# First rows of x loaded into the x2 tiles, the first recurrent unit's loads five steps ahead of it, ps_b five steps later, a step between ps_l and ps_g

## The chip, the cores and the metric

One core of a Trainium2 chip runs the whole program in one launch. The metric is the time of one execution on the device in microseconds (us). Engines are named as in the profile: PE is TensorE (matmuls; PEld are its weight loads), DVE is VectorE, ACT is ScalarE, POOL is GpSimd, and SP is SyncE, which only issues transfers. ACT and POOL issue transfers as well.

## The reference

One layer over a sequence of 2048 frames of width 1024, in float32:

```python
h = rms_norm(x, mix_norm_g)
z = h @ w_in                       # 1024 x 3328
z_conv, z_rwkv = z[..., :1536], z[..., 1536:]
y_conv = b_gate * causal_dwconv(c_gate * x_in, conv_mix_w)      # width 3
y_rwkv = rwkv7_mixer(z_rwkv, ...)  # 8 heads of 64, state 64 x 64 per head
x = x + concat([y_conv, y_rwkv]) @ w_out
x = x + conv_glu_ffn(rms_norm(x, ffn_norm_g), ...)              # width 2816
e = rms_norm(p @ ple_w_proj, ple_norm_g)
x = x + sigmoid(rms_norm(x, ple_gate_norm_g) @ ple_w_gate) * e
out = rms_norm(x, final_norm_g)
```

The recurrence in `rwkv7_mixer` takes one frame after the other: `S = S diag(w) + (S (-kk)) (kk a)^T + v k^T`, `out = S r`. Before it come token shift, decay `w`, rate `a` and gate `g` from three small projections; behind it a norm per head, a bonus `sum(r k r_k) v`, and the product with `g`.

## The kernel before

Activations lie transposed, 128 channels by 512 frames; the sequence is cut into four groups (g) of 512 frames. Every dense product is made of three matmuls per block of 128 channels: x and the weights are split into a high part that TensorE takes exactly and a low rest (`hi`, `lo`, three of the four products). A "half" is a weight tile of 128 x 512 with its low part; 12 matmuls use it. In the first group a half comes from HBM as float32 (`raw`, two buffers), ScalarE casts it (`whl` hi, L153), GpSimd subtracts (L154), and SyncE writes both parts back to HBM (`kin`, `ku`, ...). Groups 1 to 3 read these back (L161).

The dense stream runs w_in for the four groups, and then, per group, w_out, the FFN (w_up and w_down, with a piece for the embedding between) and the gate. Beside it runs the recurrent mixer, as a generator `rwkv()`: 16 units of 128 frames (two chunks of 64). The dense generators yield after every half, and `drive` lets `rwkv()` take a step at each yield (0.85 of one in w_out and gate), from the 28th half of w_in on. TensorE's instructions are pinned to this order (`pin`). On the other engines and their issuing queues a scheduler sets the order at build time, by priority and its own account of when operands are there.

A unit has 41 steps. It loads its rows (`rwkv_load`: k, tw, ad, gd, v, r from the scratch `zs`, all issued by SyncE, then kr, sq and three small operations), projects decay and rate (ps_s, ps_a), transposes (ps_n, ps_v; VectorE makes `suv` from ps_v), cumulates the decay (ps_l), projects the gate (ps_g), builds `ari` and `bk`, multiplies them (ps_e, ps_o, with ps_k for the transposes, copied into `tok`), and inverts a triangular matrix per head in a solve of 16 pairs of VectorE instructions (L792, L796), which ends in `dn`. Its rows for unit u + 1 are loaded then. ps_b is the bonus, multiplied into v. Twenty steps behind the load follow gm_ps and x_ps, which complete the inverse, and for each chunk the state (w_ps, u_ps, s_ps, o_ps). All of ps_s to ps_y share the three PSUM buffers of `ps_p`.

Rows of x of group 0 come through `staged` (L203), whose tag "s" has three buffers. The pool `x2`, ten tiles, is used from w_out on only.

```python
RATE = 1.0
SLOW = 0.85
WRAW = 2
NLD = 3
X2 = 10
```

Of the kernel before, what the change touches and what calls it, by code (L numbers as in the profile page):

```python
# [9 lines left out]
F32 = mybir.dt.float32  # L10
# [6 lines left out]
P = 128  # L17
G = 512
# [2 lines left out]
PLE_AT = 2  # L21
HELD = 2
WAIT = 20
R_BONUS = 1
R_POST = 3
R_SCORE = 3
R_MID = 2
R_X = 2
# [34 lines left out]
def tile_trunk(  # L63
# [18 lines left out]
    nc = tc.nc  # L82
    T = xT.shape[2]

    def matmul(*args, **kw):
        return pin(nc.tensor.matmul(*args, **kw))  # L86
# [33 lines left out]
    def v(name, i, n=1):  # L120
        o, _ = VEC[name]
        return vec[:, o + i : o + i + n]
# [72 lines left out]
    def blk(k):  # L195
        return slice(k * P, (k + 1) * P)
# [4 lines left out]
    def staged(pools, src, name):  # L201
        t = pools["tmp"].tile([P, G], F32, tag="s", name=name, bufs=NLD)
        nc.sync.dma_start(out=t, in_=src)  # L203
        return t
# [84 lines left out]

    def in_row(pools, g, rows, k):  # L290
        with tc.high_priority():
            x = staged(pools, xT[k, :, g * G : (g + 1) * G], "x")
        rows.add(pools, x, v("mix_norm_g", k))

    def in_proj(pools, g, rows, nxt):
# [225 lines left out]
    def rwkv_setup(rp):  # L521
        one = rp["one"]
        S = {}
        S["wup"] = one.tile([65, G], F32, tag="wup", name="wup")
        S["aup"] = one.tile([65, G], F32, tag="aup", name="aup")
        S["gup"] = one.tile([P, G], F32, tag="gup", name="gup")
        S["tw"], S["ad"], S["ari"], S["tt"] = [], [], [], []
        for s in range(1):
            for n in ("tw", "ad"):
                t = one.tile([65, P], F32, tag=f"{n}{s}", name=f"{n}{s}")  # L530
                nc.vector.memset(t[64:65, :], 1.0)
                S[n].append(t)
            ari = []
            for par in range(2):
                t = one.tile([P, 4, 2, P], F32, tag=f"ari{par}{s}", name=f"ari{par}{s}")
                ari.append(t)
            S["ari"].append(ari)
            t = one.tile([P, 2, 4, 64], F32, tag=f"tt{s}", name=f"tt{s}")
            nc.vector.memset(t, 0.0)
            S["tt"].append(t)  # L540
        S["e_last"] = one.tile([P, 4], F32, tag="e_last", name="e_last")
        nc.vector.memset(S["e_last"], 0.0)
        S["state"] = one.tile([P, 4, 64], F32, tag="state", name="state")
        nc.vector.memset(S["state"], 0.0)
        return S

    def rest(n):
        for _ in range(n):
            yield

    def rwkv_load(rp, S, u):
        if u >= 4 * NG:
            return None
        g, off = u // 4, (u % 4) * P
        ts = slice(off, off + P)
        r_t, k_t, v_t, kr, sq = (
            rp["t"].tile([P, 4, P], F32, tag="t", name=f"{n}{u}") for n in ("r", "k", "v", "kr", "sq")
        )
        tw, ad = S["tw"][0], S["ad"][0]
        gd = rp["prep"].tile([P, P], F32, tag="gd", name=f"gd{u}")  # L560
        nc.sync.dma_start(out=k_t, in_=zs[g][:, 4:8, ts])
        nc.sync.dma_start(out=tw[0:64, :], in_=zs[g][0:64, 12, ts])
        nc.sync.dma_start(out=ad[0:64, :], in_=zs[g][64:128, 12, ts])
        nc.sync.dma_start(out=gd, in_=zs[g][:, 13, ts])
        nc.sync.dma_start(out=v_t, in_=zs[g][:, 8:12, ts])
        nc.sync.dma_start(out=r_t, in_=zs[g][:, 0:4, ts])
        kkv = v("rwkv_k_k", 0, 4)[:, :, None].broadcast_to([P, 4, P])
        nc.vector.tensor_tensor(out=kr, in0=k_t, in1=kkv, op=ALU.mult)
        nc.scalar.activation(sq, kr, AF.Square)
        nc.scalar.activation(tw[0:64, :], tw[0:64, :], AF.Tanh)  # L570
        nc.scalar.activation(gd, gd, AF.Tanh, scale=0.5)
        nc.gpsimd.tensor_scalar(gd, gd, 0.5, 0.5, op0=ALU.mult, op1=ALU.add)
        return r_t, k_t, v_t, gd, kr, sq

    def rwkv_unit(rp, S, u, loaded, following):
        pr, ch, ps_p, ps_c = rp["prep"], rp["chain"], rp["ps_p"], rp["ps_c"]
        g, off = u // 4, (u % 4) * P
# [12 lines left out]
        def hi_tt(**kw):  # L590
            urgent(tt, **kw)

        def b8(t):
            return t[:, :, None].broadcast_to([P, 8, 64])

        def r8(t):
            return t.rearrange("p (h n) -> p h n", h=8)
# [23 lines left out]
        for ct in range(4):  # L621
# [3 lines left out]
            out=ksum, in_=ps_n.rearrange("p (a h n) -> p a h n", a=4, h=2),  # L625
# [12 lines left out]
        for ct in range(4):  # L638
# [3 lines left out]
            out=mean, in_=r8(ps_v), op=ALU.add, axis=mybir.AxisListType.X  # L642
# [4 lines left out]
        for c in range(2):  # L647
            rs = slice(64 * c, 64 * c + 64)
            pair = []
            for par in range(2):  # L650
# [3 lines left out]
                    out=t[vr], in0=mean4[rs, :, par, None].broadcast_to([64, 4, 64]),  # L654
# [8 lines left out]
        for cp in range(2):  # L663
            ps = ps_p.tile([P, G], F32, tag="p", name="ps_l")
            for c in range(2):
                matmul(
                    ps[:, c * 130 : c * 130 + 130], sg[:, blk(2 * cp + c)], tri[:, 0:130],
                    start=True, stop=True,
                )
            pv = ps[:, 0:260].rearrange("p (a c i) -> p a c i", a=2, c=2)  # L670
            nc.scalar.activation(ep[:, 2 * cp : 2 * cp + 2], pv, AF.Exp, scale=-DECAY)
            nc.scalar.activation(em[:, 2 * cp : 2 * cp + 2], pv, AF.Exp, scale=DECAY)
        ps_g = ps_p.tile([P, 4, P], F32, tag="p", name="ps_g")
        for ct in range(4):
            matmul(ps_g[:, ct, :], S["gup"][:, blk(ct)], gd, start=True, stop=True)
        g_t = big("g")
        nc.scalar.copy(g_t, ps_g)
        yield
        yield

        ari_e, ari_o = S["ari"][s]
# [2 lines left out]
        def cv(t):  # L684
# [9 lines left out]
            out=b_t, in0=tha, scalar=1.0, in1=kr, op0=ALU.add, op1=ALU.mult  # L694
        )
        b4 = cv(b_t)
        for rs, cs in ((E, lo), (O, hi)):
            nc.vector.scalar_tensor_tensor(
                out=bk[rs, :, :, cs], in0=b4[rs], scalar=0.5, in1=em[rs, :, :, 1:65],
# [23 lines left out]

        yield from rest(R_SCORE)
        arb, tok = [], []
# [38 lines left out]
        for pq in range(4):  # L764
            q = pq % 2
            nc.scalar.dma_start(
                out=ld[pq].rearrange("c a i j -> i c a j"),
                in_=ltt[32 * pq : 32 * pq + 32, :, :, 32 * q : 32 * q + 32],
            )
        lm = ch.tile([P, 32, 32], F32, tag="lm", name=f"lm{u}", bufs=1)  # L770
        for r in range(4):
            eng = nc.sync if r % 2 else nc.scalar
            eng.dma_start(
                out=lm[r:P:4].rearrange("m i j -> m (i j)"),
                in_=ld.rearrange("q c a i j -> (q c a) (i j)"),
# [13 lines left out]
        for i in range(0, 32, 2):  # L789
# [3 lines left out]
                out=pd[:, :, :, 0:n], in0=xs[:, :, None, 0:n].broadcast_to([P, 8, 2, n]),  # L793
# [3 lines left out]
                out=xs[:, :, i : i + 2], in_=pd[:, :, :, 0:n], op=ALU.add,  # L797
# [4 lines left out]
            out=xd.rearrange("q n r c i -> (q n r) (c i)"),  # L802
            in_=xs.rearrange("p c i -> p (c i)"),
        )
        dt_ = ch.tile([P, 8, 32], F32, tag="dt", name=f"dt{u}", bufs=1)
        for pq in range(4):
            eng = nc.sync if pq % 2 else nc.scalar
            eng.dma_start(
                out=dt_[32 * pq : 32 * pq + 32], in_=xd[pq].rearrange("n r c i -> (r c) n i")
# [10 lines left out]
        following[0] = rwkv_load(rp, S, u + 1)  # L820
        yield from rest(R_BONUS)
        ps_b = ps_p.tile([P, 4, P], F32, tag="p", name="ps_b")
# [3 lines left out]
        tt(out=v_t, in0=ps_b, in1=v_t, op=ALU.mult)  # L826
        yield from rest(WAIT - R_BONUS)
        gm_ps = ps_c.tile([P, 8, 32], F32, tag="c", name="gm_ps")
# [87 lines left out]
        hi_tt(out=r8(of), in0=r8(of), in1=b8(rs_), op=ALU.mult)  # L916
        yield from rest(R_POST)
        ps_y = ps_p.tile([P, 4, P], F32, tag="p", name="ps_y")
# [13 lines left out]
    pools, rp = {}, {}  # L932
# [13 lines left out]
    S = rwkv_setup(rp)  # L946

    def rwkv():
        following = [None]
        for u in range(4 * NG):  # L950
            loaded = following[0] or rwkv_load(rp, S, u)
            following[0] = None
            yield from rwkv_unit(rp, S, u, loaded, following)
            marks["done"] = u
# [4 lines left out]
    def in_next(g):  # L959
        def run(k):  # L960
            if g < NG and k < KD:
                in_row(pools, g, rows["in", g], k)
        return run

    def out_next(g):
# [5 lines left out]
        return run  # L971

    side = rwkv()
    debt = [0.0]

# [96 lines left out]
```

## Time and profile before

| | |
|---|---|
| median of 3 runs | 2910.98 us (2908.33 to 2916.8) |
| the profiled execution | 2920.32 us |
| its span, first to last instruction | 2918.5 us |
| mean granted clock of TensorE in it | 0.979 of 2.4 GHz |
| first matmul of w_in for group 1 | 194.91 us after the start |

The span is 2 us shorter than the execution's own time. All positions in the trace are microseconds from the start of the span. Matmuls overlap: a matmul of 512 columns is shown as 0.39 us long, but the next one starts sooner than it ends. A clock of 0.50 is the lower of TensorE's two levels, 1.2 GHz.

### The profile page before, as it was taken

To read this page: it belongs to the slowest core of one execution; us is meant where nothing else is said; L and a number is where in the kernel's file an instruction comes from. 1 tells how busy PE (TensorE), PEld (TensorE's weight loads), DVE (VectorE), ACT (ScalarE), POOL (GpSimd) and SP (SyncE) were. 2 spreads that over 40 slices of the span, in tenths; PEclk is the share of its full clock that TensorE was granted. 3 is DMA by queue.
4 is the path that set the end of the run, shared out by engine and by line. 5 is a ranking of instruction groups with operands and counts; after the bars stand their busy time and mean duration, and the time that the engine had idled before them with its cause. 6 is when DMAs were issued, how large, how long until landed. Compare 5 with 4: busy or idle time off the path is not lost.

```text
span 2918.5 us, 42094 instructions
## 1 busy us (share of the span) xinstructions
PE 2771.0 (95%) x15464; PEld 2231.7 (76%) x15464; DVE 1894.1 (65%) x3039; ACT 962.9 (33%) x1721; POOL 1109.2 (38%) x1700
## 2 busy tenths in 40 slices
PE   8899999999889999889999999999999999999997
PEld 6678788778677777667778887777788877788885
DVE  4476656648586768696676677866676856544446
ACT  4333132313453433352513123434222233411113
POOL 4533232324555565552333333323333332333321
PEclk9999999999999999989999999999999999999998
DMA  8787767777776776668665665766665658766665
GB/s 296 263 271 224 231 212 225 208 222 257 243 257 234 239 246 225 229 224 265 188 188 163 193 186 177 227 208 192 186 191 171 183 175 280 220 195 194 190 186 168
DMA packets 285803, 629.97 MB, mean 216 GB/s; under 512 B 60186, under 2 KB 113690, under 8 KB 285596
## 3 DMA queue, kind: packets, MB, share of 16 engines
q0 software_dynamic: 95040, 346.07, 39.4%
q1 hardware_dynamic: 134144, 232.83, 24.4%
q10 hardware_dynamic: 56412, 48.36, 5.2%
q8 instruction: 123, 2.02, 0.3%
q14 instruction: 84, 0.69, 0.1%
HBM read 467.77 MB, written 159.38 MB: 215 GB/s over the span
## 4 chain that ended last, share of the span: by engine, by line
PE 49%; DVE 20%; DMA 16%; ACT 5%; issue 5%; POOL 3%; ACTq 1%; SPq 0%; DVEq 0%; POOLq 0%
PE ps_mm L86 33%; PE ps_d L86 11%; DVE uf L415 3%; DVE pd L792 3%; DMA rawu<-in_w_up 2%; DMA lm<-ld 2%; DVE xs L796 2%; DMA rawin<-in_w_in 2%; DMA x<-in_xT 1%; DVE zb L255 1%; DMA ld<-ltt 1%; DMA xd<-xs 1%; PE o_ps L86 1%; DMA dt<-xd 1%; DMA es<-e 1%
## 5 line engine op out<-in xcount | busy, mean ns | idle before, releaser
L86 PE MATMUL ps_mm<-hi,whlu 128*128 128x512 f32 x2816 | 912.5, 398 | 6.0 <-ACT hi L214 4.2
L86 PEld LDWEIGHTS ps_mm<-hi,whlu 128*128 128x128 f32 x2816 | 535.0, 190 | 123.8 <-ACT hi L214 5.0
L86 PE MATMUL ps_mm<-lo,whlu 128*128 128x512 f32 x1408 | 554.2, 394 | 4.8 <-DVE lo L215 4.8
L86 PE MATMUL ps_mm<-hi,whlin 128*128 128x512 f32 x1664 | 541.7, 399 | 14.9 <-ACT whlin L153 6.9
L86 PE MATMUL ps_d<-hi,whld 128*128 128x512 f32 x1408 | 457.7, 397 | 13.8 <-DVE zb L255 5.9
L86 PEld LDWEIGHTS ps_mm<-hi,whlin 128*128 128x128 f32 x1664 | 316.1, 190 | 87.0 <-ACT whlin L153 6.9
L415 DVE SCALAR_TENSOR_TENSOR uf<-zb,vec,uf 128x512 f32<-128x512 f32 x352 | 291.7, 831 | 111.6 <-ACT uf L410 100.8
L86 PE MATMUL ps_mm<-lo,whlin 128*128 128x512 f32 x832 | 328.3, 395 | 1.6 <-DVE lo L215 1.6
L86 PEld LDWEIGHTS ps_d<-hi,whld 128*128 128x128 f32 x1408 | 266.4, 189 | 77.7 <-DVE x L455 7.0
L410 ACT ACTIVATE uf<-zb,vec 128x512 f32<-128x512 f32 x176 | 143.1, 815 | 526.8 <-DVE zb L255 481.3
L86 PEld LDWEIGHTS ps_mm<-lo,whlu 128*128 128x128 f32 x1408 | 268.0, 190 | 60.3 <-DVE lo L215 6.0
L161 POOL DMA_DIRECT2D whlu<-ku x264 | 141.8, 537 | 422.9 <-PE ps_mm L86 278.3
L86 PE MATMUL ps_d<-lo,whld 128*128 128x512 f32 x704 | 276.3, 392 | 0.0
L255 DVE TENSOR_TENSOR zb<-ps_mm,rstd 128x512 f32<-128x512 f32 x216 | 148.3, 687 | 174.9 <-PE ps_mm L86 174.1
L455 DVE TENSOR_TENSOR x<-ps_d,x 128x512 f32<-128x512 f32 x192 | 131.3, 686 | 139.3 <-PE ps_d L86 138.6
L86 PEld LDWEIGHTS ps_mm<-lo,whlin 128*128 128x128 f32 x832 | 158.1, 190 | 36.8 <-DVE lo L215 5.2
L86 PE MATMUL ps_mm<-hi,whlo 128*128 128x512 f32 x512 | 164.1, 399 | 7.9 <-DVE x L396 5.9
L86 PE MATMUL ps_mm<-hi,whlg 128*128 128x512 f32 x512 | 168.8, 405 | 0.0
L161 POOL DMA_DIRECT2D whlin<-kin x156 | 84.1, 540 | 221.0 <-PE ps_mm L86 182.8
L154 POOL TENSOR_TENSOR whlu<-rawu,whlu 128x512 fp32r<-128x512 f32 x88 | 120.0, 1364 | 109.5 <-ACT whlu L153 102.6
L154 POOL TENSOR_TENSOR lo<-th,hi 128x512 fp32r<-128x512 f32 x88 | 115.6, 1314 | 103.0 <-ACT hi L153 102.4
L86 PEld LDWEIGHTS ps_d<-lo,whld 128*128 128x128 f32 x704 | 133.5, 190 | 25.9
(205 smaller groups left out, 4237.9 us busy)
## 6 DMA issues: line engine op xcount, KB each, us to landing
whlu<-ku POOLq DMA_DIRECT2D x264, 512.0 KB, 4.4
whlin<-kin POOLq DMA_DIRECT2D x156, 512.0 KB, 4.8
whld<-kd POOLq DMA_DIRECT2D x132, 512.0 KB, 4.1
ku<-whlu SPq DMA_DIRECT2D x88, 512.0 KB, 4.4
kin<-whlin SPq DMA_DIRECT2D x52, 512.0 KB, 4.9
whlo<-ko POOLq DMA_DIRECT2D x48, 512.0 KB, 5.5
whlg<-kg POOLq DMA_DIRECT2D x48, 512.0 KB, 4.4
rawu<-in_w_up SPq DMA_DIRECT2D x88, 256.0 KB, 3.5
```

What stands on the lines that cost most here:

```text
L86: return pin(nc.tensor.matmul(*args, **kw))
L154: nc.gpsimd.tensor_tensor(out=lo, in0=raw, in1=hi.bitcast(F32), op=ALU.subtract)
L161: nc.gpsimd.dma_start(out=t, in_=kept[key])
L255: nc.vector.tensor_tensor(out=zb[:, 2 : G + 2], in0=ps, in1=rstd, op=ALU.mult)
L410: nc.scalar.activation(u, zb[:, 2 : G + 2], AF.Identity, bias=v("ffn_conv_b", n), scale=v("ffn_conv_w", 88 + n),)
L415: nc.vector.scalar_tensor_tensor(out=u, in0=zb[:, d : d + G], scalar=v("ffn_conv_w", 44 * d + n), in1=u, op0=ALU.mult, op1=ALU.add,)
L455: nc.vector.tensor_tensor(out=x2[m], in0=ps, in1=x2[m], op=ALU.add)
L792: tt(out=pd[:, :, :, 0:n], in0=xs[:, :, None, 0:n].broadcast_to([P, 8, 2, n]), in1=lm[:, None, i : i + 2, 0:n].broadcast_to([P, 8, 2, n]), ...
L796: nc.vector.tensor_reduce(out=xs[:, :, i : i + 2], in_=pd[:, :, :, 0:n], op=ALU.add, axis=mybir.AxisListType.X,)
```

## The change

Four edits. `R_BONUS` goes from 1 to 6: ps_b comes six steps behind the load of the next unit instead of one; the 20 steps up to gm_ps stay. `yield` between ps_l and ps_g: the two steps that followed ps_g are now one between and one behind. Group 0's rows of x go into eight tiles of `x2`, half issued by ScalarE, half by SyncE. `rwkv()` loads unit 0 first and then rests for five steps, so that every unit comes five steps later.

```diff
--- before.py
+++ after.py
@@ -21,8 +21,9 @@
 PLE_AT = 2
 HELD = 2
 WAIT = 20
-R_BONUS = 1
+R_BONUS = 6
 R_POST = 3
+R_FIRST = 5
 R_SCORE = 3
 R_MID = 2
 R_X = 2
@@ -289,7 +290,12 @@
 
     def in_row(pools, g, rows, k):
         with tc.high_priority():
-            x = staged(pools, xT[k, :, g * G : (g + 1) * G], "x")
+            src = xT[k, :, g * G : (g + 1) * G]
+            if g == 0:
+                x = pools["x2"].tile([P, G], F32, tag="x2", name=f"x0_{k}")
+                (nc.scalar if k % 2 else nc.sync).dma_start(out=x, in_=src)
+            else:
+                x = staged(pools, src, "x")
         rows.add(pools, x, v("mix_norm_g", k))
 
     def in_proj(pools, g, rows, nxt):
@@ -670,12 +676,12 @@
             pv = ps[:, 0:260].rearrange("p (a c i) -> p a c i", a=2, c=2)
             nc.scalar.activation(ep[:, 2 * cp : 2 * cp + 2], pv, AF.Exp, scale=-DECAY)
             nc.scalar.activation(em[:, 2 * cp : 2 * cp + 2], pv, AF.Exp, scale=DECAY)
+        yield
         ps_g = ps_p.tile([P, 4, P], F32, tag="p", name="ps_g")
         for ct in range(4):
             matmul(ps_g[:, ct, :], S["gup"][:, blk(ct)], gd, start=True, stop=True)
         g_t = big("g")
         nc.scalar.copy(g_t, ps_g)
-        yield
         yield
 
         ari_e, ari_o = S["ari"][s]
@@ -946,7 +952,8 @@
     S = rwkv_setup(rp)
 
     def rwkv():
-        following = [None]
+        following = [rwkv_load(rp, S, 0)]
+        yield from rest(R_FIRST)
         for u in range(4 * NG):
             loaded = following[0] or rwkv_load(rp, S, u)
             following[0] = None
```

On PE, the start of unit 0 behind w_in's matmuls, before (names are output and inputs, whlin the weight half):

```order
L86 MATMUL ps_mm<-hi,whlin_0_1005 128x512
L86 MATMUL ps_l<-c_tri,s_951 128x130 x4
L86 MATMUL ps_g<-gd_937,gup 128x128 x4
L86 MATMUL ps_mm<-hi,whlin_1_1012 128x512
L86 MATMUL ps_mm<-lo,whlin_1_1012 128x512
L86 MATMUL ps_mm<-hi,whlin_1_1012 128x512 x2
L86 MATMUL ps_mm<-lo,whlin_1_1012 128x512
```

and in the changed kernel:

```order
L87 MATMUL ps_mm<-hi,whlin_1_1081 128x512
L87 MATMUL ps_l<-c_tri,s_1056 128x130 x4
L87 MATMUL ps_mm<-hi,whlin_0_1166 128x512
L87 MATMUL ps_mm<-lo,whlin_0_1166 128x512
L87 MATMUL ps_mm<-hi,whlin_0_1166 128x512 x2
L87 MATMUL ps_mm<-lo,whlin_0_1166 128x512
...
L87 MATMUL ps_mm<-hi,whlin_0_1166 128x512
L87 MATMUL ps_g<-gd_937,gup 128x128 x4
L87 MATMUL ps_mm<-hi,whlin_1_1173 128x512
```

ps_g has moved behind a whole half (whlin_0_1166), and the unit itself behind five more halves of w_in (row 285 there, row 330 here).

On DVE, around the solve of unit 0 before (fold and lm prepare the matrix, pd and xs are the pairs):

```order
L761 STREAM_TRANSPOSE ltt_1294<-lt_1188 128x512
L826 TENSOR_TENSOR v_934<-ps_b,v_934 128x512
...
L781 TENSOR_TENSOR fold_1305<-lm_1300,c_sq 128x512
L783 TENSOR_TENSOR fold_1305<-fold_1305,lm_1300 128x512
...
L784 TENSOR_TENSOR lm_1300<-lm_1300,fold_1305 128x16x32
L255 TENSOR_TENSOR zb<-ps_mm,xin 128x512
L792 TENSOR_TENSOR pd<-xs_1311,lm_1300 128x16x2
L796 TENSOR_REDUCE xs_1311<-pd 128x8x2
L792 TENSOR_TENSOR pd<-xs_1311,lm_1300 128x16x4
```

and in the changed kernel:

```order
L787 TENSOR_TENSOR fold_1444<-lm_1439,c_sq 128x512
L789 TENSOR_TENSOR fold_1444<-fold_1444,lm_1439 128x512
L790 TENSOR_TENSOR lm_1439<-lm_1439,fold_1444 128x16x32
...
L798 TENSOR_TENSOR pd<-xs_1450,lm_1439 128x16x2
L802 TENSOR_REDUCE xs_1450<-pd 128x8x2
L832 TENSOR_TENSOR v_934<-ps_b,v_934 128x512
L798 TENSOR_TENSOR pd<-xs_1450,lm_1439 128x16x4
L802 TENSOR_REDUCE xs_1450<-pd 128x8x2
```

The product of ps_b with v stood ahead of fold; it now stands behind the first pair, so inside the solve. In the other 15 units it lies between the fold and the seventh pair.

On SP, the first transfers before (rawin is a raw weight half, kin the halves written back):

```order
L203 DMA x<-in_xT 128x512
L168 DMA rawin_0_228<-in_w_in 128x512
L203 DMA x<-in_xT 128x512
L168 DMA rawin_1_235<-in_w_in 128x512
L203 DMA x<-in_xT 128x512
L788 DMA xs_1311<-in_c_tri 128x256
L203 DMA x<-in_xT 128x512
L168 DMA rawin_0_269<-in_w_in 128x512
L171 DMA kin_0_232<-whlin_0_227 128x1024
L203 DMA x<-in_xT 128x512
```

and in the changed kernel (rows named x without a number are already group 1's):

```order
L296 DMA x_0_156<-in_xT 128x512
L204 DMA x<-in_xT 128x512
L169 DMA rawin_0_228<-in_w_in 128x512
L204 DMA x<-in_xT 128x512
L296 DMA x_2_173<-in_xT 128x512
L169 DMA rawin_1_235<-in_w_in 128x512
L204 DMA x<-in_xT 128x512
L296 DMA x_4_191<-in_xT 128x512
L296 DMA x_6_209<-in_xT 128x512
L169 DMA rawin_0_269<-in_w_in 128x512
L172 DMA kin_0_232<-whlin_0_227 128x1024
```

SyncE issues four of group 0's rows among the first nine transfers, with three rows of group 1 between them; the other four are issued by ScalarE.

## Rows read from the trace of the kernel before

**Rows 1.** The page, busy time: us, share of the span, instructions.

```profile
PE 2771.0 (95%) x15464; PEld 2231.7 (76%) x15464; DVE 1894.1 (65%) x3039; ACT 962.9 (33%) x1721; POOL 1109.2 (38%) x1700
```

**Rows 2.** Waits of PE, whole span: us in total, times, longest.

```profile
PE ps_g L86 <- DVE suv L653: 11.0, 7, 3.3
PE ps_n L89 <- ACT sq L569: 10.9, 1, 10.9
PE ps_b L86 <- ACT tok L755: 8.8, 4, 3.8
PE ps_o L86 <- DVE arb L752: 7.8, 5, 4.0
```

**Rows 3.** Windows by stage from 194.9 us to the end, their sum.

```profile
sum 2723.60, PE 2605.57 PEld 2101.84 DVE 1785.22 ACT 884.14 POOL 1018.52; mean PE 200.43 PEld 161.68 DVE 137.32 ACT 68.01 POOL 78.35
```

**Rows 4.** Timeline of ACT, 4 to 26 us: start, us, instruction, idle before.

```profile
5.08 0.63 ACT L227 ACTIVATE sq<-x 128x512 f32<-128x512 f32 x1 [2.61 <-DMA x<-in_xT]
...
15.85 0.63 ACT L227 ACTIVATE sq<-x 128x512 f32<-128x512 f32 x1 [3.83 <-DMA x<-in_xT]
...
23.14 0.71 ACT L214 ACTIVATE hi<-x,vec 128x512 fp32r<-128x512 f32 x1
```

**Rows 5.** The chain that ended last, 95 to 130 us: start, us, what.

```profile
101.15 3.33 DMA rawin<-in_w_in
...
115.51 4.43 DMA v<-zs
```

**Rows 6.** Timelines of SP, POOL and PE, 55 to 195 us.

```profile
55.00 0.33 SPq L168 DMA_DIRECT2D rawin<-in_w_in  x1
...
98.53 0.33 SPq L168 DMA_DIRECT2D rawin<-in_w_in  x1
...
97.22 1.28 POOL L154 TENSOR_TENSOR whlin<-rawin,whlin 128x512 fp32r<-128x512 f32 x1 [0.78 <-ACT whlin L153]
...
98.82 0.39 PE L86 MATMUL ps_mm<-hi,whlin 128*128 128x512 f32 x1
...
194.91 0.47 PE L86 MATMUL ps_mm<-hi,whlin 128*128 128x512 f32 x1 [1.65 <-DMA whlin<-kin]
```

**Rows 7.** Windows: length, busy us (instructions) by engine, granted clock, DMA, GB/s.

```profile
10.00:20.00 10.00, 6.49 (x12) 3.27 (x12) 6.36 (x9) 5.13 (x9) 2.71 (x2) 1.00 0.89 311
...
70.00:80.00 10.00, 10.00 (x45) 8.26 (x44) 3.61 (x4) 3.74 (x6) 5.71 (x7) 1.00 0.89 311
...
120.00:130.00 10.00, 9.92 (x47) 8.53 (x48) 5.66 (x12) 2.63 (x8) 2.10 (x3) 0.83 0.39 125
...
98.40:193.30 94.90, 79.06 (x365) 63.32 (x363) 65.50 (x97) 34.49 (x67) 44.08 (x45) 0.91 0.79 261
```

**Rows 8.** Timelines of PE and DVE, one window: unit 9 at ps_g.

```profile
1437.26 1.74 PE L86 MATMUL ps_g<-gd,gup 128*128 128x128 f32 x8 [3.17 <-DVE suv L653]
...
1448.96 0.69 DVE L711 TENSOR_TENSOR bk<-km,em 64x512 f32<-64x512 f32 x1
...
1454.47 0.37 PE L86 MATMUL ps_e<-ari,bk 64*128 64x128 f32 x1
...
1437.60:1441.00 3.40, 3.40 (x14) 2.92 (x13) 1.86 (x4) 3.26 (x11) 0.00 (x0) 0.50 0.68 237
```

**Rows 9.** Timelines of PE and DVE, one window: unit 5 at ps_b.

```profile
848.91 0.80 PE L86 MATMUL ps_b<-pbh,hones 128*128 128x512 f32 x1 [3.78 <-ACT tok L755]
...
848.90:853.90 5.00, 4.99 (x12) 3.93 (x13) 4.83 (x10) 0.62 (x1) 2.42 (x4) 0.50 0.75 268
...
905.29 0.45 DVE L812 STREAM_TRANSPOSE dn<-dt 128x256 f32<-128x256 f32 x1 [6.97 <-DMA dt<-xd]
...
908.39 0.69 PE L86 MATMUL gm_ps<-dn,lt 32*32 32x32 f32 x32
```

**Rows 10.** Groups by line: busy us, mean ns of one, idle before.

```profile
L792 DVE TENSOR_TENSOR pd<-xs,lm 128x32 f32<-128x32 f32 (+15 forms) x256 | 139.7, 546 | 5.5 <-POOL lm L786 0.9
...
L796 DVE TENSOR_REDUCE xs<-pd 128x16 f32<-128x32 f32 (+15 forms) x256 | 110.6, 432 | 5.2
```

## The prediction

> **What bounds the kernel now.** The page first: TensorE (PE) is busy for 2771.0 of 2918.5 us [rows 1], and its queue keeps the order in which the program was written, so every microsecond that its head waits is added to the time; the other engines matter only where they make it wait. Then the waits of PE by what ended them. The reader should see that three of them belong to places that the diff touches: ps_g, 11.0 us in seven waits, ps_n, 10.9 us in one, ps_b, 8.8 us in four [rows 2]. Then the busy time by stage: after 194.9 us PE is idle for 2723.6 - 2605.6 = 118 us [rows 3]; ps_g and ps_b hold 20 of them, many scattered waits the other 98. The granted clock in such rows shows a second price: behind a long wait PE runs for some microseconds at 0.50, its 1.2 GHz level [rows 8, 9]. Last, the start: ScalarE takes up the first row of x at 5.08 us, stands idle 3.83 us for the load of the fifth, and is done with the eighth at 23.85 us [rows 4]; those loads wait for one of the three "s" buffers.
>
> **First rows of x.** In the change all eight loads are out by about 10 us. What then limits is ScalarE's own order: eight squares of 0.63 us, eight "hi" of 0.71 us, three casts of a weight half ahead of the last "hi" (same size, taken at 0.63), three issues of about 0.33 us: 10.7 + 1.9 + 1.0 = 13.6 us after 5.08, so the last row is ready near 19 us instead of 23.85 [rows 4, 6]. That is 5 us at the first product. I book **nothing** for it. The chain that ended last runs at about 100 us not over PE but over the loop of the weights: a raw half is loaded (3.33 us there), cast, subtracted on GpSimd (1.28 us), and only then comes the next load, as there are two raw buffers [rows 5, 6]. From 55.00 to 98.53 us SyncE issues 15 halves, 2.90 us each [rows 6]; PE's 45 matmuls in 10 us [rows 7] make 2.67 us for the 12 of a half. So PE eats up its lead, and at the 29th half none is left: the subtraction ends at 98.50 us, PE reads what it wrote at 98.82 [rows 6]. A PE that begins 5 us earlier meets the same loop earlier, and the loop begins no earlier: ScalarE now casts the third and fourth halves behind rows of x. Bounds: 5 us won, 2 lost.
>
> The loads also go over two issuing queues now. An issue takes SyncE 0.33 us [rows 6], so four fewer save it 1.3 us, and between 10 and 20 us the DMA engines were 0.89 busy already [rows 7]. The Trainium skill ("DMA: Bandwidth & Descriptors", section "Issuing engines are not separate DMA queues") says that engines which issue DMAs bring no bandwidth of their own, and that issuing on several saves only issue time. By that rule the split is worth at most the 1.3 us; by the rows the wait for buffers that goes is worth 5 us at the first product and none at the 29th half, so the sum is the same by both.
>
> **First recurrent unit.** Its loads stay at the 28th half of w_in, and the unit begins five halves later. Before, PE stood 10.9 us ahead of ps_n [rows 2], and then some 2 us more ahead of ps_v, whose v was issued at 115.51 us and landed 4.43 us later [rows 5]. In the new order k and v each stand two raw loads earlier on SyncE, and PE comes five halves, 13.4 us, later: more than the 13 us of wait. From 98.4 to 193.3 us PE works off 24 halves with 94.9 - 79.1 = 15.8 us idle, at a mean clock of 0.91; in 120 to 130 us the clock was 0.83 and the DMA engines had fallen to 0.39 [rows 7]. A clock of 0.91 over 94.9 us is 17 us at half speed, most of it while PE stood; I count 7 us of work at half speed, 3.5 us lost. Without both, PE would end near 174. The weights allow 98.5 + 24 x 2.90 = 168, plus thirteen loads of 256 KB (k, v and r of two units, rows of x for the next group) at 0.8 us (estimate from the 311 GB/s of [rows 7]): 178. I take 177, a gain of **16 us**. Bounds: 20 if the weights keep up, 6 if those loads count twice (3.3 us a half).
>
> **A step between ps_l and ps_g.** ps_g needs a PSUM buffer that VectorE's (DVE's) instructions suv free. One more half of dense work, 2.67 us, covers a wait of 3.17 us nearly whole. The steps up to ps_e are as many as before, so PE comes there earlier by what it did not wait. In the unit at 1437 us the last bk ends at 1449.65 and ps_e starts at 1454.47, a slack of 4.8 us [rows 8]: nothing is given back there. Three of these waits are followed by a stretch like the 3.4 us at 0.50 in [rows 8], half of each lost: 5 us. So 11.0 + 5 = 16 at most; 5 if the evacuations behind ps_e, for which ps_o waits 7.8 us now [rows 2], take the rest. I book **12**, a microsecond given back in each of four units.
>
> **ps_b five steps on.** It waits for the copy tok; 13.4 us later that is long done. That is 8.8 us, and half of the 5.0 us at 0.50 behind the longest wait [rows 9], 11.3 together. Next late is gm, which needs dn: in that unit dn ends at 905.74 and gm starts at 908.39, so of the 3.78 us only 2.65 are kept [rows 9]. I take off 2.3 in all and book **9** (4 to 11).
>
> The product of ps_b with v moves too, from ahead of the triangular solve on VectorE into it: about 0.69 us (VectorE's time for such a size in [rows 8]) in a chain of 16 pairs of 546 + 432 ns [rows 10]. In the unit of [rows 9] gm has 2.65 us of slack; three or so have none. **2 us lost** (0 to 11, 16 x 0.69, if none had).
>
> **All units five steps later.** By counting steps, no unit is run out of turn: the last of each four still ends before its rows are asked for. But all 16 now lie 13.4 us later against the dense stages, and the 98 us of other waits are dealt anew. No row says which way: 0, with 12 us to either side (an eighth).
>
> Sum: -16 - 12 - 9 + 2 = -35 us. The profiled execution took 2920.3 us, its span 2918.5; the median of the runs, 2911.0, lies 9 us lower, and I take the same 35 us off it: **2876 us**.
>
> **Rivals.** (1) The weights hold PE: at 3.3 us a half the unit's one wait turns into many small ones, and 16 becomes 6: 2886 us. For it: no lead at 98.5 us. Against: the DMA engines' share of 0.39 in 120 to 130 us [rows 7], time that the loop gets back once PE no longer stands. (2) The waits move: VectorE is the late one at ps_g, and what PE gains it loses at ps_o and gm; 21 shrinks to 7: 2890 us. For it: ps_o's 7.8 us; against it, the slacks of 4.8 and 2.65 us. (3) Slower: the solve, 16 x 0.98 = 15.6 us of VectorE per unit [rows 10], slides by 13.4 us from the w_out stage into the start of the FFN, where PE waits for the norm and for the lo of the last row. At the three such starts with a unit running, 15.6 us and 1.7 us of clock each make 52: 2911 - 35 + 52 = 2928 us. It decides from 12 us at each start. Against: VectorE's order mixes dense instructions between the pairs, and a pair lasts 1 us. (4) The change does little: the loads were not what held the first unit, or the weights are late and the other waits come back as well: within 9 us of 2911.
>
> **How the numbers follow.** The forecast (2862 to 2890, from the 12 us of the re-dealing) 0.58; rival (1) 0.15; (2) 0.15; (4) 0.08; (3) 0.04. A measurement of this kernel tells about 0.3%, 9 us, from no change; faster by that are the first three cases, 0.88; the same 0.08; slower 0.04. For 8 in 10 the range takes in (1), (2) and both at once, 2900, and downward the better bounds (20, 16 and 11 us) with part of the re-dealing: 2856.
>
> **What would show it.** Right: ps_n waits for less than 3 us and no 0.50 between 110 and 130 us; the first matmul of the second group's w_in near 178 us instead of 194.91 [rows 6]; ps_g and ps_b gone from the list of PE's waits; small waits of w_in's matmuls for the halves (POOL, ACT whlin) between 45 and 100 us, in which the 5 us of the start go. Wrong: a start of the second group after 188 us; more than 8 us of new waits at ps_o, ps_k and gm; waits of 5 us and more at the starts of the FFN; VectorE waiting for ps_b inside the solve.

## The result and the profile after

The changed kernel takes 2931.03 us (median of 6, 2922.94 to 2937.01), the kernel before beside it 2913.89 us (6 runs, 2908.33 to 2921.87): a ratio of 1.0059, 95% interval 1.0043 to 1.0076. It is slower by 17 us where 35 us faster was forecast. The profiled execution took 2929.27 us; its span is 9.0 us longer than that of before, so the trace shows about half of what the medians show.

The page, busy time, against [rows 1]:

```profile
PE 2775.5 (95%) x15464; PEld 2234.3 (76%) x15464; DVE 1914.6 (65%) x3039; ACT 962.5 (33%) x1721; POOL 1107.1 (38%) x1700
```

The same 15464 matmuls keep PE busy 4.5 us longer, and it is idle 4.5 us longer. VectorE, with the same 3039 instructions, is busy 20.5 us longer. The waits of PE (us in total, times, longest), to be read against [rows 2]:

```profile
PE ps_e L87 <- DVE bk L716: 26.5, 6, 7.7
PE ps_d L87 <- DVE zb L256: 13.6, 7, 2.9
...
PE gm_ps L87 <- DVE dn L818: 7.3, 2, 6.2
...
PE ps_e L87 <- ACT pbh L727: 4.5, 1, 4.5
...
PE ps_o L87 <- DVE bk L717: 3.3, 4, 1.2
...
PE ps_g L87 <- issue: 1.3, 1, 1.3
...
PE ps_g L87 <- DVE suv L659: 0.8, 1, 0.8
```

The three waits at which the edits aimed are gone or nearly gone: ps_n 10.9, ps_b 8.8, ps_g 11.0 to 2.1. In their place stands one that was 1.2 us before: ps_e for `bk`, 26.5 us, the next stop of a unit behind ps_g. The waits of gm_ps for `dn` have grown from 1.4 us, and those of ps_d, a product of w_down, for `zb` from 5.9. Windows (length; busy us and instructions of PE, PEld, DVE, ACT, POOL; clock; DMA; GB/s) from the second group to the end, and of the stretch ahead of it:

```profile
188.06:2927.50 2739.44, 2610.76 (x14762) 2106.16 (x14762) 1808.41 (x2883) 883.99 (x1584) 1016.14 (x1597) 0.98 0.67 210
98.40:188.00 89.60, 81.52 (x377) 64.98 (x375) 62.48 (x88) 34.75 (x67) 45.47 (x45) 0.96 0.87 288
```

The second group begins at 188.06 us instead of 194.91 [rows 6], 6.9 us won, and the stretch ahead of it runs at a clock of 0.96 instead of 0.91 [rows 7]. From there to the end it takes 2739.4 us where it was 2723.6 [rows 3]: 15.8 us lost, 10.7 of them idle time of PE (128.7 against 118.0). Most of this is lost early: w_out of group 0 begins at 707.4 us instead of 703.4, so 10.8 of the 15.8 us go in w_in of groups 1 to 3. One wait there is new, for the end of unit 1's solve:

```profile
355.56 0.64 PE L87 MATMUL gm_ps<-dn,lt 32*32 32x32 f32 x16 [6.23 <-DVE dn L818]
```

### The profile page after: what moved, and what is told of

Its sections match the earlier page's. It is cut to its first block, busy times and chain, and to the rows that moved or that the text cites. A ratio compares the mean times of both kernels' runs of the same rounds, so it can differ in the third digit from the quotient of the medians.

```text
span 2927.5 us, 42080 instructions
## 1 busy us (share of the span) xinstructions
PE 2775.5 (95%) x15464; PEld 2234.3 (76%) x15464; DVE 1914.6 (65%) x3039; ACT 962.5 (33%) x1721; POOL 1107.1 (38%) x1700
## 4 chain that ended last, share of the span: by engine, by line
PE 40%; DVE 14%; DMA 8%; issue 3%; ACT 3%; POOL 2%; ACTq 0%; SPq 0%; DVEq 0%; POOLq 0%
PE ps_mm L87 24%; PE ps_d L87 12%; DVE uf L421 2%; DMA rawu<-in_w_up 2%; DVE pd L798 1%; DMA rawd<-in_w_down 1%; PE ps_e L87 1%; DVE xs L802 1%; DMA out<-o 1%; DMA y<-ys 1%; POOL whlu L155 1%; DVE sq L230 1%; PE o_ps L87 1%; DMA ld<-ltt 1%; DVE zb L256 1%
## 5 line engine op out<-in xcount | busy, mean ns | idle before, releaser
L87 PE MATMUL ps_mm<-hi,whlu 128*128 128x512 f32 x2816 | 912.7, 398 | 14.2 <-ACT hi L215 10.7
L87 PEld LDWEIGHTS ps_mm<-hi,whlu 128*128 128x128 f32 x2816 | 535.3, 190 | 133.5 <-ACT hi L215 12.5
L87 PE MATMUL ps_mm<-hi,whlo 128*128 128x512 f32 x512 | 165.9, 401 | 10.5 <-DVE x L402 6.6
```

## The experiments

Each run gives the ratio of its time to that of the kernel before, measured in turn on the same chip. 0.1% is 2.9 us.

| run | what it is | median, us | ratio (95%) |
|---|---|---|---|
| only_x | before + rows of x at once | 2911.1 | 0.9959 (0.9943 to 0.9974) |
| only_first | before + five steps ahead of unit 0 | 2923.5 | 1.0013 (1.0000 to 1.0025) |
| only_psg | before + step ahead of ps_g | 2911.0 | 0.9961 (0.9945 to 0.9977) |
| only_psb | before + ps_b five steps on | 2923.3 | 1.0008 (0.9994 to 1.0022) |
| no_x | changed, without the rows of x | 2926.7 | 1.0048 (1.0031 to 1.0065) |
| no_first | changed, without the five steps | 2905.6 | 0.9973 (0.9956 to 0.9990) |
| no_psg | changed, without the step ahead of ps_g | 2916.6 | 1.0006 (0.9996 to 1.0016) |
| no_psb | changed, with ps_b in its old place | 2922.8 | 1.0032 (1.0020 to 1.0044) |
| x_psg | before + x + step ahead of ps_g | 2907.8 | 0.9966 (0.9952 to 0.9980) |
| all_early | changed, b, tha and km ahead of that step | 2940.5 | 1.0074 (1.0058 to 1.0090) |
| x_psg_early | x_psg, b, tha and km ahead | 2912.2 | 0.9983 (0.9969 to 0.9996) |
| all_back | changed, five steps given back by unit 4 | 2911.5 | 0.9980 (0.9966 to 0.9994) |
| late4 | no_first, five steps behind unit 3 | 2916.8 | 1.0024 (1.0009 to 1.0039) |
| late8 | no_first, five steps behind unit 7 | 2926.5 | 1.0067 (1.0047 to 1.0087) |
| first10 | changed, ten steps instead of five | 2928.9 | 1.0067 (1.0044 to 1.0089) |
| xg_back | all_back with ps_b in its old place | 2901.2 | 0.9969 (0.9953 to 0.9986) |
| all_lean | changed, fewer products in the gate | 2922.3 | 1.0013 (0.9996 to 1.0029) |
| no_first_lean | no_first, fewer products in the gate | 2901.6 | 0.9944 (0.9922 to 0.9966) |

**One part alone.** Each takes the lines of one edit of the change's diff: `in_row`; `rwkv()` with R_FIRST; the `yield`; R_BONUS.

> The kernel before with the loads of the first rows of x alone changed (all eight into the x2 tiles at once, on two queues). Theory A (as predicted: the weight loop eats what is won at the first product): no change, within 3 us, and the 29th half of w_in begins on TensorE at 98.4 us as before. Theory B (the loads at once stand ahead of the first halves of the weights, and the loop of the raw halves starts later for it): 2 to 4 us slower, and the 29th half begins near 101 us.

> The kernel before with the first unit loaded and then begun five steps on, and nothing else; all 16 units slide by five steps. Theory A (prediction): 16 us faster, with the second group's w_in beginning near 179 us, and what the slide deals anew in the later stages within 12 us of zero. Theory B (the slide puts the preparation of later units under the stretches in which VectorE has a backlog, and loses there more than the first unit gains): the second group begins at 184 to 188 us (7 to 10 us won), but the whole is 5 to 20 us slower than before, the loss being between 190 and 720 us.

> The kernel before with the step between ps_l and ps_g alone (one of the two steps behind ps_g moved ahead of it). Theory A (prediction): 12 us faster, waits at ps_g under 2 us in all, none of over 2 us new at ps_e, ps_o. Theory B (VectorE's backlog sets the moment, and TensorE only waits for it one stop later): ps_g's waits go, but at least two thirds of their 11 us come back as waits of ps_e and ps_o for bk; 0 to 4 us faster.

> The kernel before with ps_b and its product with v five steps on, alone. Theory A (prediction): 7 us faster (9 of waits and clock, 2 lost through the product of v inside the triangular solve), ps_b's waits of 8.8 us gone, gm's waits no more than 3 us longer. Theory B (the wait moves to gm, and the product inside the solve delays dn by 0.7 us and more in each unit): ps_b's waits gone, waits of gm for dn 6 us and more longer; within 3 us of before.

Two parts win 0.4% each, two do nothing that can be told. By their sum, 17 us should be won; together they lose 17. PE in only_x, then in only_first:

```profile
113.47 0.90 PE L89 MATMUL ps_n<-c_sq,sq 128*128 128x128 f32 x3 [4.19 <-ACT sq L574]
...
191.25 0.47 PE L86 MATMUL ps_mm<-hi,whlin 128*128 128x512 f32 x1 [0.77 <-DMA whlin<-kin]
```

```profile
120.03 0.60 PE L90 MATMUL ps_n<-c_sq,sq 128*128 128x128 f32 x4
125.52 1.12 PE L90 MATMUL ps_v<-c_sq,v 128*128 128x128 f32 x4 [4.88 <-ACT s L612]
...
188.60 0.47 PE L87 MATMUL ps_mm<-hi,whlin 128*128 128x512 f32 x1 [1.63 <-DVE pd L793]
```

The five steps do take the whole wait at ps_n, and win 6.3 us up to the second group, not 16: 4.9 us come back at ps_v, which waits for ScalarE's `s`. On ScalarE it stands behind casts of weight halves, one of which waited 4.73 us for its raw half. By 707.7 us, the start of w_out, only_first is 4.3 us late, so it loses 10.6 us between 190 and 708 us, where Theory B put the loss; the whole loss of 4 us lies just under Theory B's 5. The time of only_x fits neither of its theories. The rows of x win 3.7 us up to the second group by themselves, since the wait at ps_n shrinks from 10.9 to 4.2 us: the 29th half does begin 3 us later, as Theory B of only_x said, but k and v stand two raw loads earlier on SyncE's queue (k behind 32 of them instead of 34, in every run with the rows of x and in no other). Both gains are of the same wait: with both parts it is 6.9. Where the other 8 of the 12 us of only_x come from its trace doesn't show: its profiled execution, 2917.1 us, was the longest of its six.

only_psg does what was forecast, 11 us. ps_g's waits fall to 0.7 us; ps_e waits 12.5 us for tok instead of 3.2, in waits of up to 4.8 us, though the forecast had none of over 2 us there; 1.3 us are for bk. So the waits at ps_g move on in large part, and where the 11 us come from isn't shown by them alone. only_psb loses its waits of 8.8 us, and gm waits 10.0 us for dn instead of 1.4: Theory B.

**One part left out.** The changed kernel with the lines of one edit put back.

> The changed kernel with the first rows of x loaded as before through the three s buffers. Theory A (x at once costs nothing): as the changed kernel, within 3 us. Theory B (it holds up the loop of the weights by 2.6 us): 2 to 4 us faster than the changed kernel, the 29th half at 98.4 us.

> The changed kernel without the first unit's five steps: all units stand against the dense stages as they did before. Theory A (the slide is worth 16 us at the start): 10 to 16 us slower than the changed kernel, 2940 to 2948. Theory B (the slide is what loses the time): faster than before, 2895 to 2905, as ps_g and ps_b keep what they won where the units stand as before. Theory C (VectorE's backlog takes back what any moved wait wins): within 4 us of the kernel before.

> The changed kernel with ps_g straight behind ps_l again. Theory A (the step is worth 12 us): 12 us slower than the changed kernel. Theory C (the wait moves from ps_g to ps_e): within 4 us of the changed kernel; waits at ps_g back at 8 us and more, those of ps_e for bk (26.5 us in the changed kernel) smaller by about as much.

> The changed kernel with ps_b one step behind the copies to tT, as before. Theory A (worth 7 us): 7 us slower than the changed kernel. Theory C (the wait moves to gm, or the product of v delays the solve by as much): within 3 us of the changed kernel; gm's waits for dn, 7.3 us in the changed kernel, smaller by 3 us and more.

Without the five steps the kernel is faster than before: in company they cost 0.86%, 25 us, though 4 alone. The step ahead of ps_g, worth 11 us alone, costs 0.53% beside them; without it ps_g waits 12.4 us again and ps_e only 8.6 for bk, so what the step takes from ps_g comes back larger at ps_e. Neither theory of no_psg had it 15 us faster than the changed kernel. The rows of x have no effect that can be told in company. Without the change of ps_b the kernel is 0.27%, 8 us, faster, at the edge of the noise and against both theories: ps_b waits 8.4 us again and gm waits longer, not less (9.7 us instead of 7.3).

From the first matmul of ps_l to that of ps_e a unit with nothing in its way takes 15.5 us. By the timelines, in us (the last column adds what all 16 units take beyond 15.5):

| | unit 4 | 5 | 8 | 9 | 12 | 13 | sum beyond |
|---|---|---|---|---|---|---|---|
| before | 15.9 | 16.0 | 21.6 | 21.4 | 20.6 | 21.5 | 30.7 |
| only_psg | 16.9 | 15.5 | 21.5 | 16.4 | 19.1 | 17.4 | 18.3 |
| only_first | 17.7 | 18.4 | 29.8 | 17.8 | 20.0 | 17.1 | 35.7 |
| no_first | 16.6 | 15.6 | 21.0 | 18.4 | 19.1 | 16.4 | 18.6 |
| all_back | 16.1 | 15.5 | 20.4 | 17.2 | 19.1 | 16.5 | 18.4 |
| changed | 20.1 | 22.7 | 28.7 | 17.9 | 25.0 | 17.9 | 43.9 |
| late4 | 15.5 | 23.1 | 29.4 | 17.9 | 23.0 | 18.3 | 36.7 |
| late8 | 16.2 | 15.5 | 25.9 | 18.6 | 23.1 | 17.9 | 28.7 |
| first10 | 19.4 | 19.4 | 22.1 | 17.1 | 26.8 | 15.6 | 30.1 |
| no_psg | 18.8 | 18.5 | 30.9 | 17.3 | 20.4 | 17.1 | 42.0 |
| all_lean | 19.6 | 21.8 | 23.5 | 17.5 | 19.6 | 17.3 | 31.1 |

The step ahead of ps_g alone takes 12.4 off the sum, about its gain of 11 us, and with the units five steps later the sum is 25 higher, as many us as the five steps cost. But the sum doesn't give a run's time: no_psg has almost the changed kernel's sum and is 15 us faster, and late4, with a sum 8 above that of late8, is 12 us faster than it. Units 8 and 12 prepare at the gate stages, unit 4 at the end of w_in and unit 5 in the FFN. Unit 8, VectorE's timeline in the changed kernel, from the last suv to the last bk:

```profile
1280.93 2.68 DVE L497 TENSOR_TENSOR gt<-raw,rstd 128x512 f32<-128x512 f32 x2
...
1289.96 1.72 DVE L659 SCALAR_TENSOR_TENSOR suv<-mean,ps_v 64x256 f32<-64x256 f32 x4
1291.70 0.69 DVE L501 SCALAR_TENSOR_TENSOR gt<-gt,e 128x512 f32<-128x512 f32 x1
1292.31 0.69 DVE L493 TENSOR_TENSOR e<-e,rstd 128x512 f32<-128x512 f32 x1
...
1300.69 1.78 DVE L699 SCALAR_TENSOR_TENSOR b<-tha,kr 128x512 f32<-128x512 f32 x1
1302.39 1.79 DVE L230 TENSOR_TENSOR sq<-sq 128x512 f32<-128x512 f32 x1
...
1305.29 0.74 DVE L504 SCALAR_TENSOR_TENSOR x<-gt,pg_h,x 128x512 f32<-128x512 f32 x1
1305.95 0.68 DVE L497 TENSOR_TENSOR gt<-ps_mm,rstd 128x512 f32<-128x512 f32 x1
...
1312.39 0.68 DVE L497 TENSOR_TENSOR gt<-ps_mm,rstd 128x512 f32<-128x512 f32 x1
1312.99 1.16 DVE L716 TENSOR_TENSOR bk<-km,em 64x512 f32<-64x512 f32 x1
1314.18 0.69 DVE L717 TENSOR_TENSOR bk<-km,em 64x512 f32<-64x512 f32 x1
```

PE's row behind it, and then the window from suv to bk:

```profile
1314.30 0.76 PE L87 MATMUL ps_e<-ari,bk 64*128 64x128 f32 x2 [7.72 <-DVE bk L716]
```

```profile
1291.70:1314.90 23.20, 15.36 (x70) 12.58 (x70) 22.99 (x27) 10.65 (x25) 14.96 (x12) 0.90 0.64 211
```

The same unit without the five steps (no_first): VectorE's timeline, then the window:

```profile
1258.34 1.75 DVE L492 TENSOR_TENSOR e<-e,rstd 128x512 f32<-128x512 f32 x1
...
1264.97 1.54 DVE L698 SCALAR_TENSOR_TENSOR b<-tha,kr 128x512 f32<-128x512 f32 x1
...
1270.22 1.67 DVE L716 TENSOR_TENSOR bk<-km,em 64x512 f32<-64x512 f32 x1
...
1279.91 1.28 DVE L496 TENSOR_TENSOR gt<-raw,rstd 128x512 f32<-128x512 f32 x2
```

```profile
1257.60:1271.90 14.30, 14.30 (x63) 11.64 (x63) 14.09 (x17) 9.77 (x25) 8.21 (x7) 0.89 0.46 151
```

The reader should see where gt, the gate's first product, stands. It can't start before the gate's norm is there, at 1280.93 and 1279.91 us. Without the five steps the unit's last bk is done 8 us ahead of it (ps_e starts at 1277.83 us and waits for nothing), and 17 instructions of VectorE lie between suv and bk, 14 of them the unit's. With them the unit's preparation begins 11 us behind it, and 27 lie there, 13 of them the gate's (gt, e, x, sq). VectorE is busy for 22.99 of 23.20 us.

**By stage.** That wait of 7.7 us lengthens its stage little: the first gate stage takes 68.0 us in the changed kernel and 65.6 in no_first. The three gate stages together (a fourth ends the kernel), changed and then no_first:

```profile
sum 178.70, PE 162.20 PEld 131.15 DVE 137.97 ACT 87.69 POOL 85.62; mean PE 54.07 PEld 43.72 DVE 45.99 ACT 29.23 POOL 28.54
```

```profile
sum 179.10, PE 161.01 PEld 129.17 DVE 143.35 ACT 86.09 POOL 79.41; mean PE 53.67 PEld 43.06 DVE 47.78 ACT 28.70 POOL 26.47
```

They are no longer in the changed kernel: the wait for bk stands where no_first has other waits. All stages, in us between first matmuls, in one execution of each version, which can lie 8 us off its median:

| | to the second group | w_in, groups 1 to 3 | w_out, four | FFN, four | gate, three | last gate |
|---|---|---|---|---|---|---|
| before | 194.9 | 508.5 | 189.5 | 1779.3 | 180.7 | 65.6 |
| only_psg | 197.4 | 507.8 | 193.0 | 1764.9 | 180.9 | 65.8 |
| only_first | 188.6 | 519.1 | 203.4 | 1766.4 | 178.3 | 65.4 |
| no_first | 190.7 | 509.4 | 189.5 | 1770.0 | 179.1 | 65.1 |
| all_back | 188.3 | 514.8 | 190.7 | 1765.0 | 177.3 | 65.6 |
| late4 | 188.3 | 506.9 | 194.6 | 1773.5 | 179.1 | 65.8 |
| late8 | 190.8 | 510.7 | 197.4 | 1775.1 | 189.6 | 65.2 |
| changed | 188.1 | 519.3 | 196.7 | 1778.6 | 178.7 | 65.9 |

Between no_first and the changed kernel lie 9.9 us in w_in, 7.2 in w_out and 8.6 in the FFN. The cost in w_out is in every trace in which units 8 to 15 stand later: 194.6 us and more in ten of them, 193.3 and less in the other ten. In the FFN the step ahead of ps_g alone wins 14.4 us and the five steps alone 12.9, but the changed kernel, which has both and two edits more, 0.7: there the parts don't add. Why w_out and w_in take longer isn't shown.

**Is it the order or the place?** all_early and x_psg_early move b, the scaling of tha and km; all_back shortens three waits ahead of gm:

```diff
@@ all_early, x_psg_early, behind the exponentials of ps_l
+        b_t = big("b")
+        nc.vector.scalar_tensor_tensor(out=b_t, in0=tha, ...)
+        for ct in range(4): nc.scalar.activation(tha[:, ct, :], ...)
+        km = big("km")
+        tt(out=km, in0=tha, in1=k_t, op=ALU.mult)
         yield
         ps_g = ps_p.tile([P, 4, P], F32, tag="p", name="ps_g")
@@ all_back, xg_back
-        yield from rest(WAIT - R_BONUS)
+        yield from rest(WAIT - R_BONUS - (2, 0, 2, 1)[u] if u < 4 else WAIT - R_BONUS)
```

> The kernel before with the two parts that won alone (first rows of x at once, 12 us; step between ps_l and ps_g, 11 us). Theory A (the two lie apart and add up): 20 to 24 us faster than before, ratio 0.992 to 0.993. Theory B (each deals the waits of the later stages anew, and what either won there is in part the same microseconds; the version with ps_b moved as well won 8 us only): 8 to 13 us faster, ratio 0.9955 to 0.997.

> The changed kernel with b, the scaling of tha and km, which need nothing of ps_g, written ahead of the step that now lies before ps_g, straight behind the exponentials. Theory A (the step before ps_g puts them 3 to 8 us later on VectorE and ScalarE, and so the last bk): waits of ps_e for bk fall from 26.5 us to under 12, and the kernel is 10 to 16 us faster than the changed kernel, 2915 to 2921. Theory B (VectorE has that much work in these stretches whatever its order): waits of ps_e stay above 20 us, and the time within 4 us of the changed kernel.

> First rows of x at once, the step before ps_g, and b, tha and km ahead of that step; units where they stood before. Theory A (where the units stand as before, the last bk has 1 to 6 us of slack ahead of ps_e, so its lateness costs nothing): within 4 us of the version without the early b. Theory B (the lateness costs there too): 5 us and more faster than it.

> The changed kernel, but units 0, 2 and 3 wait 2, 2 and 1 steps less ahead of gm, so that the five steps are given back by unit 4 and all units from there on stand against the dense stages as before. Theory A (the five steps later lose the time in the stages from w_out on): 2899 to 2907, as the version without the five steps (2905.6) or a little faster. Theory B (the loss lies in the first four units or in something else than the place of the units): above 2920.

x_psg: Theory B; the gains of two parts don't add up. all_early refutes Theory A in its price: the wait for bk is gone, and the kernel is no faster than the changed one. The waits of PE in all_early:

```profile
PE ps_d L87 <- DVE x L461: 17.2, 9, 5.3
PE ps_e L87 <- ACT tok L761: 14.7, 7, 3.7
```

ps_d waited 4.6 us for x in the changed kernel. So the waits have moved from the unit to the dense stream. x_psg_early wins nothing over x_psg. all_back is as fast as no_first, as Theory A said, 23 us faster than the changed kernel (0.9980 against 1.0059), and its sum is 18.4: where the units stand from w_out on decides most of the loss. In the traces 21 of the 26 us between the two lie behind the start of w_out.

```diff
@@ late4 (u == 3), late8 (u == 7), both on no_first, behind each unit
             marks["done"] = u
+            if u == 3:
+                yield from rest(5)
@@ first10
-R_FIRST = 5
+R_FIRST = 10
@@ all_lean, no_first_lean
                 e = staged(pools, es[g][:, m, :], "e")
-                nc.vector.tensor_tensor(out=e, in0=e, in1=re, op=ALU.mult)
...
-                nc.vector.tensor_tensor(out=th, in0=ps, in1=rstd, op=ALU.mult)
...
-                nc.scalar.activation(th, th, AF.Tanh, scale=0.5)
+                nc.scalar.activation(th, ps, AF.Tanh, scale=0.5)
```

> The changed kernel without the five steps at the first unit, but with five steps of dense work more behind unit 3, so that units 4 to 15 stand where they stand in the changed kernel and units 0 to 3 where they stood before. Theory A (the place of units 4 to 15 is the loss): from the first matmul of ps_l to that of ps_e, TensorE then takes 20 to 24 us longer over units 4 to 15 than in the version without the five steps; 2925 to 2932, 20 to 26 us slower than that version. Theory B (the loss comes from the first unit's own delay, or from a kernel-wide effect of another order): within 5 us of that version, 2901 to 2911.

> As the run with five more steps behind unit 3, but behind unit 7: units 8 to 15 alone stand five steps later. Theory A (each unit pays at its own place, the two at the gate stages, 8 and 12, most): 14 to 16 us slower than the version without the five steps, about 2920. Theory C (what one unit loses the next wins back, so where the slide begins doesn't matter): as the run with the steps behind unit 3.

> The changed kernel with ten steps ahead of the first unit in place of five. Theory A (a unit's preparation is slow where VectorE has the gate's products or the FFN's evacuations at the same time, and ten steps leave units 8 and 12 wholly within the gate stage): no better than the changed kernel, 2925 to 2940. Theory D (five steps hit a bad place by chance, and any other number is as good as none): 2900 to 2915.

> First rows of x at once, the step before ps_g, the first unit five steps later, and the five steps given back in units 0, 2 and 3; ps_b where it was before. Theory A (the first unit's delay is worth the 2 to 4 us that the start of the second group shows, and the rest is as without it): 2 to 5 us faster than x and ps_g alone, ratio to before 0.995 to 0.9965. Theory B (the three units that wait less ahead of gm lose as much): ratio 0.9965 to 0.998.

The delay of units 8 to 15 alone brings the kernel to 1.0067, the whole of the loss, 27 us over no_first where Theory A allowed 16; that of units 4 to 15 costs 15 us, less than its 20 to 26, and its sum grows by 18 where Theory A had 20 to 24. So the place of the later units is the cause, but the price of a place can't be added up unit by unit. In late8 alone of the runs with five steps the gate stages are longer, by 10.5 us. Ten steps are as bad as five. xg_back: Theory B; the first unit's own delay is worth nothing that can be told over x_psg.

> The changed kernel with two of VectorE's five products of each gate column left out: e is not scaled by its norm, and the gate's row is not scaled ahead of the tanh, which ScalarE takes straight from the product. So 64 products of 0.69 us are not computed and the output is another. Theory A (units 8 and 12 are late because their preparation meets VectorE's products of the gate): from ps_l to ps_e unit 8 takes 16 to 21 us in place of 28.7, unit 12 16 to 20 in place of 25.0, and the kernel is 12 us and more faster than the changed kernel. Theory B (something else holds these units, such as ScalarE or the order): unit 8 stays above 25 us and unit 12 above 22.

> The same two products left out of each gate column in the version without the five steps. Theory A (there the preparation of units 8 and 12 is over before the gate's products begin): unit 8 from ps_l to ps_e 18 to 21 us (21.0 with the products), unit 12 17 to 19 (19.1); at most 6 us faster than with them, and the distance between the two versions, 0.86% with the products, falls to under 0.6%. Theory B: the distance stays at 0.8% or more.

With fewer products of the gate on VectorE, unit 12 falls from 25.0 to 19.6 and unit 8 from 28.7 to 23.5 us, and unit 8 stays above Theory A's 21; the changed kernel gains 0.46%, 13 us, the one without the five steps 0.29%, 8 us, above the 6 allowed. The distance between them falls from 0.86% to 0.69%, between the two theories; each of the two distances is known to about 0.25%, so the fall isn't clear of noise. So the gate's products are shown to hold units 8 and 12 (the two products left out also spare ScalarE a wait); they are not shown to be any large part of the 25 us, and the gate stages themselves, late8's aside, are as long with the five steps as without. Units 4 and 5 stay late (19.6 and 21.8).

## Why the prediction was wrong

**First rows of x, booked at 0.** The mechanism was right up to the 29th half: PE is 2.1 us ahead at the second half (15.02 instead of 17.15), not 5, and the loop of the weights takes it back; the 29th half starts at 100.98 us instead of 98.36, 2.6 lost, just outside the bound. But alone the edit wins 12 us, 3.7 of them up to the second group, where the scheduler put k and v two raw loads earlier, a move that the prediction gave to the five steps. In the changed kernel SyncE issues k here (before at 106.95, behind two more halves) and v at 110.66 instead of 115.51 [rows 5]:

```profile
105.29 0.43 SPq L567 DMA_DIRECT2D k<-zs  x1
...
110.66 0.42 SPq L571 DMA_DIRECT2D v<-zs  x1
```

**First recurrent unit, booked at 16.** The mechanism was right: no wait at ps_n, and a clock of 1.00 between 110 and 130 us. The size was not: 6.9 us up to the second group with the rows of x, 6.3 alone, and only 2.6 beside them (188.06 against 190.70 us in no_first). The start at 188.06 us meets the prediction's own sign of being wrong, 188. Alone, 4.9 us of the wait come back at ps_v; in the changed kernel the unit waits again at ps_g, ps_e and ps_o, 4.3 us in all, and the clock is 0.52 from 146 to 153 us.

**Step between ps_l and ps_g, booked at 12.** Right alone (11 us, the sum down by 12.4), wrong in company. That "nothing is given back there" at ps_e rested on a slack of 4.8 us in one unit of before [rows 8]; with the five steps PE waits for bk in six units.

**ps_b, booked at 9 less 2.** The waits went and gm's came: 10.0 us in only_psb. That was the mechanism of rival (2), at gm alone. In company the change costs 8 us, at the edge of the noise.

**All units five steps later, booked at 0 with 12 to either side.** This step failed and turned the sign: it cost 25 us in company (no_first against the changed kernel), twice its bound. (The forecast's range, 2862 to 2890, is 14 us to either side of 2876, not the 12 named for it.) No reason was given for taking it at 0, and "No row says which way" was not so for ps_e: VectorE's timeline of the kernel before, at the first gate stage, shows the last bk of unit 8 and the first gt:

```profile
1280.71 0.69 DVE L711 TENSOR_TENSOR bk<-km,em 64x512 f32<-64x512 f32 x1
1286.32 1.29 DVE L491 TENSOR_TENSOR gt<-raw,rstd 128x512 f32<-128x512 f32 x2
```

The unit was done 4.9 us ahead of the burst, and a delay of five steps is 13.4 us. PE's waits at ps_e are 18.3 us in all in no_first and 35.3 in the changed kernel; the 17.0 between them are as much as PE's idle time differs by in the whole span (135.1 and 152.0, span less busy). That is partly chance, since the other waits change too: in the gate stages PE is idle no longer than in no_first, and in w_in of groups 1 to 3 it is idle 7 us longer, with the one wait of 6.2 us for dn.

Rival (3) gave nearly the right time, 2928 us, mostly by luck: its waits of 12 us at the starts of the FFN didn't come (the longest is 4.7 us). The solve does slide into a busy stretch once, at unit 1 in w_in; elsewhere it is the preparation ahead of the solve that is late. What stays open: through which waits the later place of the units costs its time in w_in and w_out, why late8 loses more than late4, and where only_x wins most of its 12 us. That the delay costs only 4 us alone goes with the 12.9 us that it wins in the FFN there; why it wins them isn't shown. No version that computes everything is shown to be faster than only_x and only_psg, each 0.4%; their combinations are no better.

## What to carry to other kernels

Before work is slid against another stream, look at what the shared engine does in the stretch that it will slide into, not only at the wait that goes: here VectorE's burst of gate products has a fixed start, and the work fitted ahead of it. Where VectorE was busy for 22.99 of 23.20 us, taking away a wait of TensorE, or reordering, moved the wait to another stop. A new long wait is not yet a loss: compare the length of its stage, since the wait can stand where another stood. Parts that each win alone can be paid from the same slack: measure them together, and leave each out once.

## What the runs showed of the hardware

VectorE's products of two operands in SBUF, of 512 columns, took 0.68 to 0.70 us while GpSimd stood; beside its work some took as long, and many 1.6 to 1.8 us. Unit 5 of the changed kernel, VectorE and then GpSimd:

```profile
843.37 0.68 DVE L718 TENSOR_TENSOR ari<-r,ep 64x512 f32<-64x512 f32 x1
...
856.89 1.74 DVE L716 TENSOR_TENSOR bk<-km,em 64x512 f32<-64x512 f32 x1
858.66 1.64 DVE L717 TENSOR_TENSOR bk<-km,em 64x512 f32<-64x512 f32 x1
```

```profile
856.38 1.71 POOL L155 TENSOR_TENSOR whlu<-rawu,whlu 128x512 fp32r<-128x512 f32 x1
858.05 1.71 POOL L155 TENSOR_TENSOR whld<-rawd,whld 128x512 fp32r<-128x512 f32 x1
859.72 1.72 POOL L728 TENSOR_TENSOR pbl<-pb,pbh 128x512 fp32r<-128x512 f32 x1
```

The two engines' instructions end in turn, and VectorE's price for the same work depends on what GpSimd does beside it; this may be a part of the 20.5 us that VectorE is busy longer over the kernel. No run took GpSimd's work away, so its share isn't measured. The Trainium skill ("SBUF — State Buffer", section "SBUF: two separate sides") says that these two engines share a pair of ports under an exclusive lock, which an instruction of VectorE with two inputs in SBUF takes part in; the rows agree, and a product with an operand in PSUM, unit 8's gt at 1312.39 us, took 0.68 us beside an instruction of GpSimd from 1311.89 to 1313.61.
